# Attention block with Winograd-form projections on one core: when the small scale vectors are loaded, when the sums of staged tokens fall due, who scales B21 and B22, and the order of the products where output units change and end

## The chip, the cores and the metric

The kernel runs on 1 core of one Trainium2 chip, as one launch. The metric is the device time of a run in microseconds (us); less is better. The five engines are called by the names of the profile: PE (TensorE, matmuls), DVE (VectorE), ACT (ScalarE), POOL (GpSimd) and SP (SyncE, which issues most transfers).

## The reference, cut to what matters

One layer over x of 512 tokens by 2048 channels:

```
h    = rms_norm(x, norm_g)
proj = h @ w_in                     # 2048 x 8192: qa ka va ga | qb kb vb gb
ya   = stick_breaking_attention(qa, ka, va)          # 8 heads of 128, strictly causal
yb   = chunk_band_attention(qb, kb, vb, q_norm_g, k_norm_g, rel_bias)   # 8 heads, QK-norm
mixed = concat(ya * silu(ga), yb * silu(gb))
x    = x + mixed @ w_out            # 2048 x 2048
```

The channel gain norm_g is multiplied into x before the projection; the token's factor (1/rms) is multiplied in after it, as the row vector R.

## The kernel before

**Products.** All float32 values go to PE as two rounded parts, high and low, and each product is three matmuls (`three`, L463 to L465: high by high, then the two mixed ones). The projection is cut into 32 units of 256 columns; a unit walks the 2048 channels in 4 steps (`steps_`; a step has two channel tiles of 128, so tokens j = 2r and 2r+1). The output stage is 4 more units (NU to NU+3) of 8 steps, each with two token halves a = 0 and 1. Units 0 and 1, and unit NU, are PLAIN: 8 products of a 2x2 block scheme for each step. All others take 7 products in Winograd's form (`WINOGRAD`), which need sums of weights (`sums`, L331 to L335) and sums of tokens (T1 to T4, L428 to L433). The first eight steps are unit 0 and 1 in turn: steps 0, 1 read tokens j = 0, 1; steps 2, 3 read j = 2, 3; steps 4, 5 read j = 4, 5; steps 6, 7 read j = 6, 7. Unit 2 begins with step 8, and it is the first to read T1 to T4.

**Staging of tokens.** `activations(j)` loads tokens j into one of four stage tiles (`STAGE[j % 4]`, named cq, ck, cv, cg; j + 4 waits until the four sums of j have been read out of it), as two transfers: B11 with B12, and B21 with B22. `raw` scales each piece by the channel gain `ng_t` (ACT, L446), `raw_split` makes the high part (ACT, L457) and the low part (DVE, L458). Then the sums are made in one tile `xt` (L428, L430, L431) and split (L432, L433).

**Weights.** `step_weights(n)` loads the two 256 KB halves of step n (L292) into one of three buffers; `split` makes the high part on ACT (L351, `wh`) and the low part on DVE (L355, `wl`), in two buffers each: the high part of step n waits until PE has passed step n - 2. Part 0 has 1024 columns, part 1 (the sums) 768.

**Statistics and head scales.** `x_stats` loads x again in 16 tiles of 256 KB (L727) and squares them on ACT (L732); R follows from it. `constants` loads the head gains qg_t and kg_t (L1067, L1068) and scales qg_t on DVE (L1071).

**Order.** Every engine's order is written out at build time: an event loop (`schedule`) holds a clock and a cost for each operation, and each engine that is free takes the ready operation with the earliest due time. `need(k, d)` is due d us before PE would reach product k. On the chip each engine runs its list in order, so one instruction that waits holds all behind it.

**Ends of units.** `combine` puts a unit's seven sums together: copy of halves 0 and 1 to U (ACT, L606), then on DVE L613, L615, L617 (512 wide), L618, L617, L618; in the last unit (NU+3) also the residual x from `xres` (four operations of 256 between). Each of these frees a PSUM half-bank, and PE's next unit waits for those that it writes. In the output stage the two halves use fixed banks, so unit u + 1 writes where unit u has just been summed. The last two steps of NU+3 run, for each a, first 7 products of step 6, then 7 of step 7 (order `LAST`).

Of the kernel before, what the change touches and what calls it, by code (L numbers as in the profile page):

```python
# [8 lines left out]
F32 = mybir.dt.float32  # L9
# [6 lines left out]
P = 128  # L16
# [40 lines left out]
def trunk_kernel(ctx: ExitStack, tc: tile.TileContext, xT, xn, wi, wqk, wo, ng, qg, kg, rel, out):  # L57
# [189 lines left out]
    for n, (u, r) in enumerate(steps_):  # L247
        names = PLAIN if plain(u, r) else LAST if r == (NR if u < NU else NJ) - 1 else WINOGRAD
        if n == 0:

            for kk in range(2):
                put(n, 0, [x + ((kk,),) for x in names])
        elif u < NU:
            put(n, 0, names)
        elif u == NU + 3 and r > NJ - 3:

            if r == NJ - 1:
                for a in range(2):
                    for n_ in (n - 1, n):
                        put(n_, a, names if n_ == n else WINOGRAD)  # L260
        elif r in (0, NJ - 1):

            for a in range(2):
                put(n, a, names)
        else:
            for x in names:
                for a in range(2):
                    put(n, a, (x,))
# [118 lines left out]
    def activations(j, mixed):  # L387

        if mixed:
            g = j // 2 * 2  # L390
            yield lambda: (("store", g, j % 2) in done and ("store", g + 1, j % 2) in done
                           and position[0] > at_step[step_of[NU - 1, j // 2]] + 6)
            yield lambda: all(emptied(t_, NG - 1) for t_ in STAGE[:2]) if j % 2 == 0 else ("scores", 2 * NG - 1) in done
            k = at_step[step_of[NU, j]]
            kt = at_step[step_of[NU + plain(NU, j), j]]
        else:
            k = at_step[step_of[0, j // 2]] + (len(PLAIN) if j == 1 else 0)
            kt = at_step[step_of[2, j // 2]]
        lot = ("stage", j % 2 if mixed else j % 4)
# [23 lines left out]
        if not mixed:  # L423
# [4 lines left out]
        yield DV(512, lambda: dve.tensor_tensor(out=two(t[:, :2 * H]), in0=r[:, None, 3 * H:].to_broadcast([P, 2, H]),  # L428
                                               in1=two(r)[:, 0:3:2, :], op=ALU.subtract), need(kt, 4))
        yield DV(256, lambda: dve.tensor_tensor(out=t[:, 2 * H:3 * H], in0=t[:, :H], in1=r[:, 2 * H:3 * H], op=ALU.subtract), need(kt, 4))  # L430
        yield DV(256, lambda: dve.tensor_tensor(out=t[:, 3 * H:], in0=t[:, 2 * H:3 * H], in1=r[:, H:2 * H], op=ALU.add), need(kt, 4))  # L431
        yield AC(1024, lambda: act.copy(f(h[:, 3:]), t), need(kt, 2.6))  # L432
        yield DV(1024, lambda: dve.tensor_tensor(out=f(l[:, 3:]), in0=t, in1=f(h[:, 3:]).bitcast(F32), op=ALU.subtract), need(kt, 0.5))  # L433
        done.update(("x", j, x, mixed) for x in ("T1", "T2", "T3", "T4"))
# [6 lines left out]
    def raw(j, mixed, load_, r, k, parts, channels, scaled):  # L441
        yield load_
        if scaled:
            for x in parts:
                s_ = r[:, x[0] * H:x[1] * H]
                yield AC((x[1] - x[0]) * H, lambda: act.activation(s_, s_, AF.Copy, scale=ng_t[:, channels:channels + 1]), need(k, 3.5))  # L446
        done.add(("scaled", j, channels, mixed))
        for x in parts:
            spawn(raw_split(j, mixed, r, k, *x), (0, 0, j))
# [136 lines left out]
    def combine(u, a):  # L586
# [27 lines left out]
        free(4)  # L614
        yield DV(256, lambda: dve.tensor_tensor(out=c[0][:, 0], in0=w[0], in1=w[1], op=ALU.add), soon(1))  # L615
        yield there(2, 3)
# [6 lines left out]
        if u == NU and PLAIN_STEPS:  # L623
            yield there(5)
            yield DV(256, lambda: add_(c[1][:, 1], c[1][:, 1], v(one(5))), soon(1))
            free(5)
        final = u == NU + 3
        if final:

            yield lambda: ("xres", a) in done  # L630
            xf = [xres[a].rearrange("p h (b f c) -> p h b f c", f=2, c=P)[:, :, :, f, :] for f in range(2)]
            where = lambda h: out[(2 * h + a) * P:(2 * h + a + 1) * P, (u - NU) * S:(u - NU + 1) * S]
            def both_x():
                sub_(w[1], w[1], xf[0][:, 1])
                add_(w[0], w[0], xf[1][:, 0])

            def add_x():
                add_(c[0][:, 0], c[0][:, 0], xf[0][:, 0])
                add_(c[1][:, 1], c[1][:, 1], xf[1][:, 1])

            yield DV(256, both_x, soon(0.5), n=2)
            yield DV(256, add_x, soon(0.8), n=2)
        yield there(6)
# [70 lines left out]
    def x_stats():  # L714
        yield lambda: position[0] > 12
        for t in range(NT):
# [340 lines left out]
    def constants():  # L1057
# [76 lines left out]
```

## Time and profile before

| what | value |
|---|---|
| time, median of 3 runs | 960.51 us (960.45 to 961.32) |
| profiled execution: its own time | 961.33 us |
| profiled execution: span from first to last instruction | 959.5 us |
| PE busy | 934.9 us, 97% |
| DVE busy | 825.2 us, 86% |
| ACT busy | 583.0 us, 61% |
| POOL busy | 19.0 us, 2% |

The profile is of one execution; times in it count from its first instruction. A matmul of 256 columns shows as 0.28 us, but the next starts 0.12 us after it, since they are pipelined: the pitch, from start to start, is what counts. In step 0 the pitch is 0.21 us.

### The profile page before, as it was taken

The page shows a single profiled execution, that of the slowest core. Times are in us where ns is not written, and L with a number is a line of the kernel's source. Part 1 is how long each engine was busy: PE and PEld are TensorE (multiplying, and loading weights), DVE is VectorE, ACT ScalarE, POOL GpSimd, SP SyncE. Part 2 cuts the span into 40 slices and gives each one's busy share as a digit, 9 for nine tenths or more (in the row PEclk, how much of TensorE's full clock was granted, in tenths as well). Part 3 has the DMA queues.
Part 4 walks back from the last instruction along what each step waited for, and adds up shares of the span by engine and source line. Part 5 has one row for each costly group of instructions (what it writes and reads, how often), then busy time and mean ns, then how long its engine had stood idle before and what let it go on. Part 6 is the DMA issues. An engine that isn't in the chain of part 4 may idle for free.

```text
span 959.5 us, 19478 instructions
## 1 busy us (share of the span) xinstructions
PE 934.9 (97%) x7592; PEld 923.2 (96%) x7592; DVE 825.2 (86%) x1519; ACT 583.0 (61%) x1104; POOL 19.0 (2%) x61
## 2 busy tenths in 40 slices
PE   5899999999999999999999999999999999999997
PEld 5899999999999999999999999999999999999997
DVE  4799998889999889889998898889989988777875
ACT  6876765865467658654776585547768666533332
POOL 0000000000000000000000000000000000101010
PEclk9999999999999999999999999999999999999998
DMA  6842233323322332133223332332322446656361
GB/s 230 261 136 78 88 110 121 100 67 111 110 90 88 116 106 88 68 132 98 89 79 122 110 100 66 120 101 88 100 88 89 144 132 202 151 195 178 110 178 45
DMA packets 63629, 112.43 MB, mean 117 GB/s; under 512 B 7216, under 2 KB 11312, under 8 KB 63536
## 3 DMA queue, kind: packets, MB, share of 16 engines
q1 hardware_dynamic: 61392, 107.51, 34.5%
q0 software_dynamic: 1728, 3.15, 2.0%
q8 instruction: 59, 0.97, 0.4%
q10 hardware_dynamic: 416, 0.52, 0.2%
q14 instruction: 34, 0.28, 0.1%
HBM read 102.77 MB, written 8.39 MB: 116 GB/s over the span
## 4 chain that ended last, share of the span: by engine, by line
PE 84%; DVE 9%; ACT 3%; DMA 2%; issue 1%; SPq 0%; DVEq 0%; ACTq 0%
PE banks L463 27%; PE banks L464 27%; PE banks L465 27%; DVE wl L355 3%; PE banks L952 2%; PE banks L880 1%; ACT wh L351 1%; DMA x<-mixd 1%; DMA wt<-in_wi 1%; PE banks L988 1%; DMA qg_t<-in_qg 1%; DVE wt L331 0%; DVE c L976 0%; DVE U L617 0%; DVE wtl L961 0%
## 5 line engine op out<-in xcount | busy, mean ns | idle before, releaser
L463 PE MATMUL banks<-xh,wh 128*128 128x256 f32 x1776 | 512.2, 288 | 9.1 <-ACT xh L457 8.3
L464 PE MATMUL banks<-xl,wh 128*128 128x256 f32 x1776 | 504.0, 284 | 5.1 <-DVE xl L458 5.0
L465 PE MATMUL banks<-xh,wl 128*128 128x256 f32 x1776 | 503.8, 284 | 0.0
L351 ACT CAST wh<-wt 128x1024 fp32r<-128x1024 f32 (+2 forms) x306 | 285.7, 943 | 255.1 <-PE banks L464 146.6
L355 DVE TENSOR_TENSOR wl<-wt,wh 128x1024 fp32r<-128x1024 f32 (+2 forms) x306 | 331.5, 1087 | 72.5 <-ACT wh L351 68.6
L463 PEld LDWEIGHTS banks<-xh,wh 128*128 128x128 f32 x1776 | 341.4, 192 | 10.3 <-ACT xh L457 8.5
L464 PEld LDWEIGHTS banks<-xl,wh 128*128 128x128 f32 x1776 | 341.6, 192 | 6.4 <-DVE xl L458 5.9
L465 PEld LDWEIGHTS banks<-xh,wl 128*128 128x128 f32 x1776 | 341.4, 192 | 0.3 <-DVE wl L355 0.3
L463 PE MATMUL banks<-wh,xh 128*128 128x256 f32 x432 | 122.7, 284 | 1.7 <-DVE co L618 1.7
L464 PE MATMUL banks<-wl,xh 128*128 128x256 f32 x432 | 122.3, 283 | 0.1
L465 PE MATMUL banks<-wh,xl 128*128 128x256 f32 x432 | 122.2, 283 | 0.0
L331 DVE TENSOR_TENSOR wt<-wt 128x512 f32<-128x512 f32 x144 | 98.1, 682 | 13.8 <-DMA wt<-in_wo 13.8
L463 PEld LDWEIGHTS banks<-wh,xh 128*128 128x128 f32 x432 | 82.9, 192 | 2.5 <-DVE co L618 2.5
L464 PEld LDWEIGHTS banks<-wl,xh 128*128 128x128 f32 x432 | 82.9, 192 | 0.3 <-DVE wl L355 0.3
L465 PEld LDWEIGHTS banks<-wh,xl 128*128 128x128 f32 x432 | 82.9, 192 | 0.0
L334 DVE TENSOR_TENSOR wt<-wt 128x256 f32<-128x256 f32 x144 | 60.3, 420 | 2.0
L335 DVE TENSOR_TENSOR wt<-wt 128x256 f32<-128x256 f32 x144 | 60.4, 419 | 2.0
L606 ACT COPY U<-banks 128x512 f32<-128x512 f32 x36 | 21.1, 585 | 25.4 <-PE banks L465 25.0
L961 DVE TENSOR_TENSOR wtl<-banks,wth 128x128 fp32r<-128x128 f32 (+1 forms) x64 | 30.8, 482 | 1.4 <-ACT wth L960 1.0
L952 PE MATMUL banks<-ident,W 128*128 128x128 f32 x160 | 28.6, 276 | 1.4 <-DVE wtl L961 0.9
L960 ACT CAST wth<-banks 128x128 fp32r<-128x128 f32 (+1 forms) x64 | 26.9, 422 | 3.2 <-PE banks L952 3.1
L617 DVE TENSOR_TENSOR U<-banks,c 128x512 f32<-128x512 f32 x30 | 20.7, 688 | 7.8 <-PE banks L465 6.1
(179 smaller groups left out, 1019.2 us busy)
## 6 DMA issues: line engine op xcount, KB each, us to landing
wt<-in_wi SPq DMA_DIRECT2D x256, 256.0 KB, 2.9
wt<-in_wo SPq DMA_DIRECT2D x64, 256.0 KB, 3.4
xs<-in_xn SPq DMA_DIRECT2D x16, 256.0 KB, 4.3
mixd<-c SPq DMA_DIRECT2D x16, 256.0 KB, 2.1
out<-co SPq DMA_DIRECT2D x16, 256.0 KB, 4.6
x<-in_xT SPq DMA_DIRECT2D x14, 256.0 KB, 5.4
co<-in_xn POOLq DMA_DIRECT2D x12, 256.0 KB, 7.2
bias<-in_rel SPq DMA_DIRECT2D x8, 256.0 KB, 3.6
```

Of the source, the lines that this page charges most:

```text
L331: yield DV(512, lambda: dve.tensor_tensor(out=some(t, 8, -7, 2), in0=some(t, 5, -5, 2), in1=some(t, 1, 0, 2), op=ALU.add), need(k0, 4))
L334: yield DV(256, lambda: dve.tensor_tensor(out=some(t, 9, 2), in0=some(t, 8, 2), in1=some(t, 0, 2), op=ALU.add), need(k1, 4))
L335: yield DV(256, lambda: dve.tensor_tensor(out=some(t, 12, 1), in0=some(t, 9, 2), in1=some(t, 4, 2), op=ALU.add), need(k1, 3.5))
L351: act.copy(whl[n, part][0][:, c], t)
L355: yield DV(c.stop - c.start, lambda: dve.tensor_tensor(out=l[:, c], in0=t, in1=h[:, c].bitcast(F32), op=ALU.subtract), need(k, 0.5))
L463: pe.matmul(o, lh, rh, start=start, stop=False, **kw)
L464: pe.matmul(o, lh, rl, start=False, stop=False, **kw)
L465: pe.matmul(o, ll, rh, start=False, stop=stop, **kw)
L606: act.copy(x[0], pair(u, a, 0, 1))
L952: pe.transpose(t[:, j * P:(j + 1) * P], src[:, j * P:(j + 1) * P], ident)
L960: yield AC(w, lambda: act.copy(th[:, blocks, :], tv))
L961: yield DV(w, lambda: dve.tensor_tensor(out=tl[:, blocks, :], in0=tv, in1=th[:, blocks, :].bitcast(F32), op=ALU.subtract))
```

## The change

Six edits:

1. `x_stats` may start when PE has passed 36 products, not 12; `constants` loads the head gains when PE has passed 40, not at once.
2. The sums of tokens j < 4 are due 8 us before the step of unit 0 that needs the stage tile again (step 4 or 6), not before unit 2.
3. B21 and B22 of tokens j = 2 to 7 in the projection are scaled by DVE (`tensor_scalar`, 512 wide), not by ACT: six instructions.
4. The first step of units NU+1 to NU+3 runs in the order `FIRST`: of each seven products those to halves 0, 1, 4, 2, 3, 7, 6, where it was 0, 1, 2, 7, 3, 6, 4.
5. The last two steps of NU+3 take turns product by product, both in the order `LAST`, for a = 0 and then a = 1.
6. At the end of NU+3, for a = 1, the sum of L615 and the residual of that quarter go to POOL (`apart`). The wait for `xres` in the builder is gone.

```
+FIRST = tuple(WINOGRAD[i] for i in (0, 1, 6, 2, 4, 3, 5))
-        names = PLAIN if plain(u, r) else LAST if r == (NR if u < NU else NJ) - 1 else WINOGRAD
+        names = PLAIN if plain(u, r) else LAST if r == (NR if u < NU else NJ) - 1 else FIRST if u > NU and r == 0 else WINOGRAD
...
                 for a in range(2):
-                    for n_ in (n - 1, n):
-                        put(n_, a, names if n_ == n else WINOGRAD)
+                    for x in LAST:
+                        for n_ in (n - 1, n):
+                            put(n_, a, (x,))
...
-            kt = at_step[step_of[2, j // 2]]
+            kt, dt = (at_step[step_of[0, j // 2 + 2]], 8) if j < 4 else (at_step[step_of[2, j // 2]], 0)
...
+                if x[2] == ("B21", "B22") and j > 1:
+                    yield DV((x[1] - x[0]) * H, lambda: dve.tensor_scalar(out=s_, in0=s_, scalar1=g_, scalar2=None, op0=ALU.mult), need(k, 3.5))
+                else:
+                    yield AC((x[1] - x[0]) * H, lambda: act.activation(s_, s_, AF.Copy, scale=g_), need(k, 3.5))
...
+        if final and a:
+            spawn(apart(c, w, xf), (0, 0))
+        else:
+            yield DV(256, lambda: dve.tensor_tensor(out=c[0][:, 0], in0=w[0], in1=w[1], op=ALU.add), soon(1))
...
             def add_x():
-                add_(c[0][:, 0], c[0][:, 0], xf[0][:, 0])
+                if not a:
+                    add_(c[0][:, 0], c[0][:, 0], xf[0][:, 0])
                 add_(c[1][:, 1], c[1][:, 1], xf[1][:, 1])
...
+    def apart(c, w, xf):
+        yield G(0.75, lambda: pool.tensor_tensor(out=c[0][:, 0], in0=w[0], in1=w[1], op=ALU.add), clock[0])
+        done.add("c11")
+        yield G(0.75, lambda: pool.tensor_tensor(out=c[0][:, 0], in0=c[0][:, 0], in1=xf[0][:, 0], op=ALU.add), clock[0])
+        done.add("c11 x")
...
-        yield lambda: position[0] > 12
+        yield lambda: position[0] > 36
...
+        yield lambda: position[0] > 40
         def gains():
```

In the sums' five operations every `need(kt, d)` became `need(kt, dt + d)`. The line numbers of the changed kernel are larger: L458 became L466, L355 became L358, L428 to L431 became L432 to L435, L615 became L629, L617 became L631, L618 became L632, L1071 became L1095.

**Where instructions moved.** DVE in step 0, before. The tile x_111 is the stage tile of tokens 0, xt_161 their sums, wl_0 the low part of step 0's weights:

```order
L428 TENSOR_TENSOR xt_161<-x_111 128x512
L1071 TENSOR_SCALAR qgs<-qg_t 128x1
L458 TENSOR_TENSOR xl_113<-x_111,xh_112 128x512
L355 TENSOR_TENSOR wl_0_143<-wt_124,wh_0_142 128x512
L430 TENSOR_TENSOR xt_161<-xt_161,x_111 128x256
L458 TENSOR_TENSOR xl_116<-x_114,xh_115 128x256
```

The scale of qg_t is second of the six. DVE in step 0 of the change:

```order
L432 TENSOR_TENSOR xt_159<-x_111 128x512
L466 TENSOR_TENSOR xl_113<-x_111,xh_112 128x512
L358 TENSOR_TENSOR wl_0_143<-wt_124,wh_0_142 128x512
L434 TENSOR_TENSOR xt_159<-xt_159,x_111 128x256
L466 TENSOR_TENSOR xl_116<-x_114,xh_115 128x256
L466 TENSOR_TENSOR xbqk_145<-x_114,xbqk_145 128x256
```

The scale of qg_t, which stood ahead of the low parts of B21 and B22 (xl_113) and of the second half of step 0's weights, has gone from here.

It stands now behind the low part of step 5's weights. DVE of the change there (xt_438 are the sums of tokens 3, xt_520 those of tokens 4, x_439 is the stage tile of tokens 6):

```order
L358 TENSOR_TENSOR wl_5_472<-wt_314,wh_5_471 128x1024
L1095 TENSOR_SCALAR qgs<-qg_t 128x1
L437 TENSOR_TENSOR xl_122<-xt_438,xh_121 128x1024
L432 TENSOR_TENSOR xt_520<-x_293 128x512
L452 TENSOR_SCALAR x_439<-x_439,ng_t 128x512
L466 TENSOR_TENSOR xl_441<-x_439,xh_440 128x256
L466 TENSOR_TENSOR xbwth_351<-x_439,xbwth_351 128x256
L434 TENSOR_TENSOR xt_520<-xt_520,x_293 128x256
```

Behind it stand the pieces of tokens 6 and 7, which step 6 reads: from the scale of qg_t to the low part of B11 of tokens 7 (exclusive) there are three instructions of 1024 columns, five of 512 and four of 256.

SP before, from step 2's weights (wt_146) on; xs is a tile of the statistics:

```order
L292 DMA wt_146<-in_wi 128x512 x2
L1067 DMA qg_t<-in_qg 128x1
L1068 DMA kg_t<-in_kg 128x1
L292 DMA wt_184<-in_wi 128x512 x2
L727 DMA xs<-in_xn 128x512
L292 DMA wt_234<-in_wi 128x512 x2
L727 DMA xs<-in_xn 128x512 x2
```

The loads of the head gains stand right behind the weights of step 2. SP of the change, from the second load of tokens 5 (x_362) to the weights of step 8 (wt_501):

```order
L420 DMA x_362<-in_xT 128x512
L295 DMA wt_417<-in_wi 128x512 x2
L749 DMA xs<-in_xn 128x512
L419 DMA x_439<-in_xT 128x2x256
L420 DMA x_439<-in_xT 128x512
L749 DMA xs<-in_xn 128x512 x2
L1091 DMA qg_t<-in_qg 128x1
L1092 DMA kg_t<-in_kg 128x1
L295 DMA wt_501<-in_wi 128x512 x2
```

The loads of the weights of steps 3 to 7 and of tokens 4 to 6 (x_293, x_362, x_439) now stand ahead of that of qg_t, and three tiles of the statistics too.

DVE at the end of NU+3, for a = 1, before:

```order
L613 TENSOR_TENSOR co_1_11764<-banks,U 128x2x128
L615 TENSOR_TENSOR co_1_11764<-U 128x2x128
L617 TENSOR_TENSOR U<-banks,co_1_11764 128x512
L618 TENSOR_TENSOR co_1_11764<-banks,U 128x2x128
L617 TENSOR_TENSOR U<-U,xres_10452 128x256
L618 TENSOR_TENSOR U<-U,xres_10452 128x256
L618 TENSOR_TENSOR co_1_11764<-co_1_11764,xres_10452 128x2x128 x2
L617 TENSOR_TENSOR co_1_11764<-banks,U 128x2x128
L618 TENSOR_TENSOR co_1_11764<-banks,U 128x2x128
```

For each a there are ten operations on DVE. In the change, the same place:

```order
L621 TENSOR_TENSOR co_1_11754<-banks,U 128x2x128
L631 TENSOR_TENSOR U<-banks,co_1_11754 128x512
L632 TENSOR_TENSOR co_1_11754<-banks,U 128x2x128
L631 TENSOR_TENSOR U<-U,xres_10451 128x256
L632 TENSOR_TENSOR U<-U,xres_10451 128x256
L632 TENSOR_TENSOR co_1_11754<-co_1_11754,xres_10451 128x2x128
L631 TENSOR_TENSOR co_1_11754<-banks,U 128x2x128
L632 TENSOR_TENSOR co_1_11754<-banks,U 128x2x128
```

Two of the ten are gone from here, L615 and one of the two that add xres to co. POOL of the change, from its last transfers on:

```order
L683 DMA co_1_10835<-in_xn 128x512 x2
L683 DMA co_0_11276<-in_xn 128x512 x2
L683 DMA co_1_11309<-in_xn 128x512 x2
L674 TENSOR_TENSOR co_1_11754<-U 128x2x128
L676 TENSOR_TENSOR co_1_11754<-co_1_11754,xres_10451 128x2x128
```

The two stand there as L674 and L676, alone behind the transfers of NU+1 and NU+2.

## Rows read from the trace of the kernel before

**Rows 1.** The page, part 1: busy us of each engine, its share of the span, and its instructions.

```profile
PE 934.9 (97%) x7592; PEld 923.2 (96%) x7592; DVE 825.2 (86%) x1519; ACT 583.0 (61%) x1104; POOL 19.0 (2%) x61
```

**Rows 2.** Who waited for whom, for PE over the whole span: total us, times, longest.

```profile
PE banks L463 <- ACT xh L457: 8.3, 2, 5.8
PE banks L464 <- DVE xl L458: 5.0, 2, 4.8
PE banks L463 <- DVE co L618: 1.7, 4, 0.6
PE banks L463 <- DVE c L617: 0.8, 1, 0.8
```

**Rows 3.** The timeline of 0 to 22 us, lines of PE, ACT, DVE and SP's queue (SPq): start, duration, engine, line, operation, and in brackets the idle time ahead of it and who ended it.

```profile
5.84 0.58 PE L463 MATMUL banks<-xh,wh 128*128 128x256 f32 x1 [5.84 <-ACT xh L457]
...
6.98 0.41 PE L465 MATMUL banks<-xh,wl 128*128 128x256 f32 x1
...
7.02 0.60 ACT L457 CAST xh<-x 128x512 fp32r<-128x512 f32 x1
...
8.52 0.33 SPq L1067 DMA_DIRECT2D qg_t<-in_qg  x1
...
9.11 0.41 PE L463 MATMUL banks<-xh,wh 128*128 128x256 f32 x1
...
13.56 0.15 DVE L1071 TENSOR_SCALAR qgs<-qg_t 128x1 f32<-128x1 f32 x1 [6.08 <-DMA qg_t<-in_qg]
13.63 0.68 DVE L458 TENSOR_TENSOR xl<-x,xh 128x512 fp32r<-128x512 f32 x1
...
14.37 0.58 PE L464 MATMUL banks<-xl,wh 128*128 128x256 f32 x1 [4.84 <-DVE xl L458]
...
19.40 0.28 PE L464 MATMUL banks<-xbqk,wh 128*128 128x256 f32 x1
...
21.07 0.28 PE L463 MATMUL banks<-xh,wh 128*128 128x256 f32 x1
```

**Rows 4.** The timeline of PE over step 4, whose first matmul is at 38.35 and which ends where step 5 begins at 48.70; and one line of the table by stretches (length, busy us of PE, PEld, DVE, ACT, POOL, then PE's granted clock, DMA share, GB/s).

```profile
38.35 0.28 PE L463 MATMUL banks<-xh,wh 128*128 128x256 f32 x1
...
41.37 0.38 PE L463 MATMUL banks<-xh,wh 128*128 128x256 f32 x1 [2.50 <-ACT xh L457]
...
48.70 0.28 PE L463 MATMUL banks<-xh,wh 128*128 128x256 f32 x1
...
43.30:46.70 3.40, 3.40 (x18) 3.40 (x18) 1.66 (x3) 3.38 (x8) 0.00 (x0) 0.50 0.95 293
```

**Rows 5.** The same table for 58 to 115 us and 140 to 200 us (same columns), and from the timeline DVE's copy that makes R.

```profile
58.00:115.00 57.00, 56.55 (x461) 55.66 (x460) 56.83 (x106) 37.74 (x71) 0.77 (x4) 1.00 0.30 93
...
140.00:200.00 60.00, 59.69 (x492) 58.99 (x491) 52.92 (x118) 38.99 (x100) 0.96 (x6) 1.00 0.32 102
...
67.70 0.68 DVE L764 COPY R<-banks 128x512 f32<-128x512 f32 x1
```

**Rows 6.** Transfers issued in 0 to 60 us: line, count, KB of each, median us from issue to landing.

```profile
x<-in_xT SPq DMA_DIRECT2D x14, 256.0 KB, 5.4
...
ng_t<-in_ng SPq DMA_DIRECT2D x1, 8.0 KB, 2.2
qg_t<-in_qg SPq DMA_DIRECT2D x1, 0.5 KB, 5.0
```

**Rows 7.** Groups of instructions with shapes kept apart: busy us, mean ns of one, idle ahead.

```profile
L458 DVE TENSOR_TENSOR xl<-x,xh 128x512 fp32r<-128x512 f32 x12 | 8.2, 685 | 0.1
...
L856 DVE TENSOR_TENSOR W<-banks,W 128x128 f32<-128x128 f32 x8 | 2.3, 286 | 0.1
...
L752 DVE TENSOR_SCALAR diag<-ident,rstd 128x128 f32<-128x128 f32 x4 | 1.2, 302 | 0.0
```

**Rows 8.** The timeline where unit NU+2 follows NU+1 (its first product is at 869.09), lines of PE and DVE; and the table by stretches for the first step and the next of NU+2, and for the first step of NU+3 (columns as in rows 4).

```profile
869.09 0.28 PE L463 MATMUL banks<-wh,xh 128*128 128x256 f32 x1
...
870.97 0.38 PE L463 MATMUL banks<-wh,xh 128*128 128x256 f32 x1 [0.64 <-DVE co L618]
...
873.96 0.39 PE L463 MATMUL banks<-wh,xh 128*128 128x256 f32 x1 [0.23 <-DVE co L618]
...
870.50 0.74 DVE L618 TENSOR_TENSOR co<-banks,U 128x256 f32<-128x256 f32 x2
...
873.50 0.41 DVE L618 TENSOR_TENSOR co<-banks,U 128x256 f32<-128x256 f32 x1
...
869.10:875.50 6.40, 5.53 (x44) 5.13 (x43) 6.26 (x13) 2.49 (x3) 2.62 (x3) 1.00 0.32 53
...
910.80:917.20 6.40, 5.54 (x45) 5.13 (x44) 6.25 (x13) 2.48 (x3) 2.63 (x3) 1.00 0.40 77
```

**Rows 9.** The timeline of the end of the run, lines of ACT, DVE and PE, and POOL's one elementwise instruction of 128 columns at the start.

```profile
950.87 0.59 ACT L606 COPY U<-banks 128x512 f32<-128x512 f32 x1 [4.45 <-PE banks L465]
...
952.35 0.28 PE L465 MATMUL banks<-wh,xl 128*128 128x256 f32 x1
...
952.51 0.69 DVE L617 TENSOR_TENSOR U<-banks,co 128x512 f32<-128x512 f32 x1
...
955.25 0.41 DVE L618 TENSOR_TENSOR co<-banks,U 128x256 f32<-128x256 f32 x1
...
1.02 0.29 POOL L1049 TENSOR_SCALAR_AFFINE_SELECT ident<-ident 128x128 f32<-128x128 f32 x1
```

More of the change, by code (lines that the diff above doesn't have):

```diff
@@ L394, in activations @@
             k = at_step[step_of[NU, j]]
-            kt = at_step[step_of[NU + plain(NU, j), j]]
+            kt, dt = at_step[step_of[NU + plain(NU, j), j]], 0
         else:
             k = at_step[step_of[0, j // 2]] + (len(PLAIN) if j == 1 else 0)
-            kt = at_step[step_of[2, j // 2]]
+            kt, dt = (at_step[step_of[0, j // 2 + 2]], 8) if j < 4 else (at_step[step_of[2, j // 2]], 0)
         lot = ("stage", j % 2 if mixed else j % 4)
@@ L428, in activations @@
         yield DV(512, lambda: dve.tensor_tensor(out=two(t[:, :2 * H]), in0=r[:, None, 3 * H:].to_broadcast([P, 2, H]),
[L429 to L433, printed above, removed]
+                                               in1=two(r)[:, 0:3:2, :], op=ALU.subtract), need(kt, dt + 4))
+        yield DV(256, lambda: dve.tensor_tensor(out=t[:, 2 * H:3 * H], in0=t[:, :H], in1=r[:, 2 * H:3 * H], op=ALU.subtract), need(kt, dt + 4))
+        yield DV(256, lambda: dve.tensor_tensor(out=t[:, 3 * H:], in0=t[:, 2 * H:3 * H], in1=r[:, H:2 * H], op=ALU.add), need(kt, dt + 4))
+        yield AC(1024, lambda: act.copy(f(h[:, 3:]), t), need(kt, dt + 2.6))
+        yield DV(1024, lambda: dve.tensor_tensor(out=f(l[:, 3:]), in0=t, in1=f(h[:, 3:]).bitcast(F32), op=ALU.subtract), need(kt, dt + 0.5))
         done.update(("x", j, x, mixed) for x in ("T1", "T2", "T3", "T4"))
@@ L445, in raw @@
                 s_ = r[:, x[0] * H:x[1] * H]
-                yield AC((x[1] - x[0]) * H, lambda: act.activation(s_, s_, AF.Copy, scale=ng_t[:, channels:channels + 1]), need(k, 3.5))
+                g_ = ng_t[:, channels:channels + 1]
+                if x[2] == ("B21", "B22") and j > 1:
+                    yield DV((x[1] - x[0]) * H, lambda: dve.tensor_scalar(out=s_, in0=s_, scalar1=g_, scalar2=None, op0=ALU.mult), need(k, 3.5))
+                else:
+                    yield AC((x[1] - x[0]) * H, lambda: act.activation(s_, s_, AF.Copy, scale=g_), need(k, 3.5))
         done.add(("scaled", j, channels, mixed))
@@ L614, in combine @@
         free(4)
-        yield DV(256, lambda: dve.tensor_tensor(out=c[0][:, 0], in0=w[0], in1=w[1], op=ALU.add), soon(1))
+        final = u == NU + 3
+        xf = [xres[a].rearrange("p h (b f c) -> p h b f c", f=2, c=P)[:, :, :, f, :] for f in range(2)] if final else None
+        if final and a:
+            spawn(apart(c, w, xf), (0, 0))
+        else:
+            yield DV(256, lambda: dve.tensor_tensor(out=c[0][:, 0], in0=w[0], in1=w[1], op=ALU.add), soon(1))
         yield there(2, 3)
@@ L626, in combine @@
             free(5)
-        final = u == NU + 3
         if final:
-            yield lambda: ("xres", a) in done
-            xf = [xres[a].rearrange("p h (b f c) -> p h b f c", f=2, c=P)[:, :, :, f, :] for f in range(2)]
             where = lambda h: out[(2 * h + a) * P:(2 * h + a + 1) * P, (u - NU) * S:(u - NU + 1) * S]
+            yield lambda: not a or "c11" in done
             def both_x():
@@ L637, in add_x @@
             def add_x():
-                add_(c[0][:, 0], c[0][:, 0], xf[0][:, 0])
+                if not a:
+                    add_(c[0][:, 0], c[0][:, 0], xf[0][:, 0])
                 add_(c[1][:, 1], c[1][:, 1], xf[1][:, 1])
             yield DV(256, both_x, soon(0.5), n=2)
-            yield DV(256, add_x, soon(0.8), n=2)
+            yield DV(256, add_x, soon(0.8), n=2 - a)
         yield there(6)
@@ L652, in combine @@
         if final:
+            yield lambda: not a or "c11 x" in done
             yield from stored(lambda: sp.dma_start(where(0), t[:, 0, :]))
```

## The prediction

> **What bounds the kernel now.** I read the page's busy times first. PE is busy 97% of the span, DVE 86%, POOL hardly [rows 1]; a change that leaves PE's products alone, as this one does, can only win PE's idle time, its time at half clock, and what lies before its first and behind its last matmul. The span is 959.5 us, the profiled execution 961.33, its median fellow 960.51; sums below are made on the span, and I carry them to the median as they stand.
>
> Then the view of who PE waited for [rows 2]. The longest, 5.8, is the first; 4.8 of the 5.0 at DVE's L458, and 2.5 (8.3 less 5.8), are two more long ones; four of 1.7 in all are for DVE at L618, and one of 0.8 for L617.
>
> *Step 0* [rows 3]. DVE sits idle 6.08 us for the 0.5 KB of qg_t, issued at 8.52, while the high part of B21 is there at 7.62. PE's last matmul ahead of the stop starts at 9.11 and takes 0.41, so it runs out at 9.5; it resumes at 14.37. Its pitch is 0.21 us until 19.40, then 0.12: the lower and the upper of the two clock levels, 1.2 and 2.4 GHz. The rise comes 5.0 us after PE resumed. Step 1 begins at 21.07, 15.23 us after the first matmul, where 48 matmuls at 0.12 are 5.76.
>
> *Step 4* [rows 4]. 38.35 to 48.70 is 10.35 us, so 4.59 are lost: 2.50 waiting for tokens 5, and then 3.4 us in which the granted clock is 0.50, about 1.7 lost; the rest is restart.
>
> *58 to 115 us* [rows 5]. DVE is busy 56.83 of 57 us there, and PE 56.55: a second engine without slack. This decides whether time won earlier can be kept.
>
> *Output stage* [rows 8]. The first step of NU+2 takes from 869.09 to 875.50, 6.41 us where 42 matmuls are 5.04, and so does that of NU+3: 1.37 lost in each. *End* [rows 9]: the last matmul starts at 952.35, DVE's last operation at 955.25, the span ends at 959.5.
>
> **Step 0: the wait removed.** qg_t's scale leaves this place, so the low part of B21 follows L428 as soon as its high part is there, at about 7.7, and the low part of the second half of the weights right behind it. PE needs the first at 9.5. So PE runs on from 5.84 at 0.21 until the clock rises. When is an estimate: 5.0 us after a resumption in step 0, 5.3 in step 4 (41.37 to 46.7) [rows 3, 4], which counted from 5.84 to 6.98 gives 10.8 to 12.3; I take 11.6. By then PE has done 2 + (11.6 - 6.98)/0.21, about 24 matmuls, and step 1 begins at 11.6 + 24 x 0.12 = 14.5 instead of 21.07: **6.5 us** (5.9 to 6.9). ACT's and DVE's lists for tokens 0 and 1 are otherwise unchanged.
>
> **Step 4.** With 14.5 for step 1, steps 2 to 6 are due at 20.3, 26.0, 31.8, 37.5, 43.3. Tokens 5 now load behind the weights of step 6 and not behind tiles of the statistics. Those weights need the buffer of step 3, whose low part waits for PE to pass step 1: two casts of 1024 columns, at most 2.4 us by twice the 512-wide ones [rows 3, 7], so 22.7; the tokens are issued at 23.7 to 24.6 and land 5.4 later by the median [rows 6], 29.1 to 30.0. Two short ACT operations and one of DVE make 31. PE asks at 32.1. The loss goes: **4.6 us**; if they land 2.5 us later it is 3, or less if the clock falls too.
>
> **The new place of qg_t.** The load stands behind the weights of step 7, which need step 4's buffer (PE past step 2 at 26.0, plus 2.4: 28.4), and six more issues of about 0.5: issued near 31.9. It lands 2.2 to 5.0 later, as ng_t and qg_t did [rows 6]: 34.1 to 36.9. DVE reaches it behind step 5's low part, 31.8 + 2.4 = 34.2. So DVE waits 0 to 2.7 us with the pieces of tokens 6 and 7 behind it. The twelve operations between cost 8 to 9 us (0.69 at 512 columns and 0.29 at 128 [rows 7], linear between and beyond, less the overlap); with no wait the low part of tokens 7 starts near 42.7, and step 6 asks for it at 43.7. A wait of 1.8, the middle, costs PE **0.8 us**; the ends are 0, and 1.8 with 1.7 of half clock as in step 4, 3.5.
>
> **Scaling by DVE, sums due earlier.** Six operations of 512 columns go to DVE. At 128 columns a tensor_scalar shows 302 ns and a two-tensor operation 286 [rows 7], so I price them like the latter, 6 x 0.69 = 4.1 us at most. They fill idle time: the wait of 6.08 is gone, and the sums of tokens 0 to 3 move into the first 40 us, which PE's slow start left idle on DVE. At nothing on the path; if that cover failed, 4.1.
>
> **Can PE stay ahead?** In 58 to 115 DVE is full [rows 5], but by what it has put off, not by what the stretch itself asks. With the 6.1 idle us at qg_t gone and R, with the first heads' work, moved behind step 12, I count DVE ahead of its weights through step 24. The 0.8 wait at L617 in that stretch [rows 2] should mostly go: **0.6** (0 to 0.8). The heads of group 0 then fall where DVE is busy 52.9 of 60 us and ACT 39.0 [rows 5]; I take **-0.3** for new short waits (0 to -2).
>
> **First steps of NU+2 and NU+3.** PE's fourth product (half 7) waits until 870.97 for the last operation of a = 0 (two L618 from 870.50), and that of a = 1 until 873.96 for the L618 at 873.50 [rows 8]. In FIRST half 7 comes sixth, two products of 0.36 later, and half 4 third, whose bank L613 freed long before. DVE's list there is the same, so its ends stay: after 873.96 two products are left, not four, and the step ends 0.72 to 0.82 earlier. Two steps: **1.6 us** (0.9 to 1.7, if DVE's ends move). NU+1 follows a unit without a combination and has no such loss.
>
> **End.** Now step 6 and 7 finish a half together every 0.72 us, counted back from PE's end E: halves 0, 1 at E - 3.6, half 4 at E - 2.16, half 3 at E - 1.44. The 512-wide L617 can start near E - 1.4, where it starts at 952.51 = E - 0.1 now, and two operations of the ten on DVE are gone, one of them behind it (0.33). That is **1.6 us** at most, and I take **1.5**. It holds if POOL is in time: L617 overwrites U, so it waits for POOL's sum, which can start at E - 2.9 when U is copied. It has 1.5 us. POOL's 128-column operation takes 0.29 [rows 9]; 256 columns with a second input lie between 0.4 and 1.2, I take 0.7, and the second sum has two more us. If it took 2.5, 1.0 would be lost.
>
> The Trainium skill speaks against this part: "GPSIMD Engine Reference", "3.1 Elementwise — side-by-side cycle accounting", has a two-input fp32 addition at about twice VectorE's time (4497 ns for 2048 columns). No run here shows a two-input operation on POOL; by that figure 256 columns are an estimated 0.6 to 0.9 us, L617 would not be delayed, and the sum stays.
>
> **Sum.** 6.5 + 4.6 - 0.8 + 0.6 - 0.3 + 1.6 + 1.5 = 13.7 us, so 945.8 of span and 946.8 at the median.
>
> **Rivals.**
>
> *A. The wait moves with the load.* qg_t lands at 37 or later, DVE stands for 3 us, PE waits 2 us or more in step 6 and the clock falls as it did in step 4. For it: the load is issued behind eight transfers of 256 KB, and landed 5.0 us late in such a crowd. Against: PE's demand there is a step later. It costs 4 more: 951. Chance 0.18.
>
> *B. DVE gives nothing back.* The full stretch [rows 5] holds PE to a lead of about 4 us, and only step 4's loss or step 0's is kept. Gain 4 + 1.6 + 1.5, less 0.5: 954. For: 56.83 of 57 busy, and 4.1 us of work added. Against: the put-off sums are done by then. Chance 0.10.
>
> *C. Slower: the heads of group 0 come too late.* R is made at 67.70 now [rows 5]; its tiles load behind step 7's, so it comes some 17 us later, near step 13. The four tiles of group 0 must be read before unit 4, 16 steps in, can be summed, or PE stands with full banks. The chain of two heads has about 15 us to spare at step 20; it decides from 15 + 13.7, that is if the chain came 29 us late. At 35 the time is 967. Chance 0.03.
>
> *D. The edits do less than they say:* the clock in step 0 rises no earlier, since the start is not dense enough, and PE runs at 0.21 through step 0 and 1 (+4 us): 951. Against: PE worked from 5.84 to 9.5 without a stop of more than a matmul's length. Chance 0.07.
>
> **How the numbers follow.** The forecast has 0.62: 946.8, its own range 943.5 (all upper ends) to 949.5. A and D at 951 add 0.25, B at 954 is left at the edge. The range **943.5 to 953** leaves out B, C and little more. About 0.2%, 1.9 us, is what a measurement of this kernel tells from no change: faster 0.94, within 0.03, slower 0.03.
>
> **What would show it.** Right: no idle time of DVE ahead of the scale of qg_t in step 0; step 1 near 14.5, step 5 near 37.5; one step of 5.5 to 5.7 us at the start of NU+2 and NU+3; from the last matmul's start to the span's end 5.6 us, now 7.2. Wrong: DVE idle over 3 us near 34 and PE with it (A); PE short of weights between steps 8 and 16 (B); waits of PE near step 20 (C); a pitch of 0.21 beyond 13 us (D); L617 waiting for POOL.

## Result, and the profile after

The changed kernel takes 948.85 us (median of 4 runs, 948.39 to 951.60) where the kernel before takes 960.62 (4 runs, 960.45 to 961.32): a ratio of 0.988, 95% interval 0.9868 to 0.9893, so 11.8 us less. The forecast was 946.8, with a range of 943.5 to 953. The profiled execution took 948.75 us, with a span of 947.0 where it was 959.5; the profiled execution before, with 961.33, was the slowest of its four, so spans differ by 0.8 us more than the medians.

The page's busy times, to hold against [rows 1]: PE's are 3.8 us less, and fewer matmuls run at the longer pitch; the other 8.7 of the span's 12.5 us were idle time of PE.

```profile
PE 931.1 (98%) x7592; PEld 920.3 (97%) x7592; DVE 827.0 (87%) x1523; ACT 579.6 (61%) x1097; POOL 20.4 (2%) x63
```

Who PE waited for, over the whole span (total us, times, longest), to hold against [rows 2]:

```profile
PE banks L471 <- ACT xh L465: 7.2, 2, 5.8
PE banks L974 <- DVE wtl L983: 0.9, 3, 0.3
PE banks L473 <- DVE wl L358: 0.8, 1, 0.8
PE banks L472 <- DVE xl L466: 0.5, 2, 0.3
PE banks L471 <- DVE co L632: 0.4, 2, 0.2
```

The waits of 4.8 for DVE's low part and of 0.8 for L617 are gone; those for L618 (now L632) shrank from 1.7 to 0.4. The ACT wait of 2.5 in step 4 is gone too; in its place stand one of 1.4 (7.2 less 5.8) and one of 0.8 for the low part of weights, and both are new and stand in step 6.

Step 0, from the timeline, PE and DVE (start, duration, engine, line, in brackets the idle time ahead and who ended it), to hold against [rows 3]:

```profile
5.83 0.58 PE L471 MATMUL banks<-xh,wh 128*128 128x256 f32 x1 [5.83 <-ACT xh L465]
...
7.65 0.69 DVE L466 TENSOR_TENSOR xl<-x,xh 128x512 fp32r<-128x512 f32 x1 [0.19 <-ACT xh L465]
...
9.52 0.41 PE L473 MATMUL banks<-xh,wl 128*128 128x256 f32 x1
...
10.80 0.29 PE L473 MATMUL banks<-xh,wl 128*128 128x256 f32 x1
...
14.16 0.28 PE L471 MATMUL banks<-xh,wh 128*128 128x256 f32 x1
```

The low part of B21 starts at 7.65, where it was 13.63. PE does not stop; its matmuls go from 0.41 to 0.28 us, and from a pitch of 0.21 to one of 0.12, at 10.8, where it was 19.4. Step 1 begins at 14.16, 6.91 earlier.

Step 5 begins at 37.20 (48.70 in [rows 4]), 11.50 earlier: step 4 loses nothing any more. Then step 6, which runs from 42.96; the lines of SP's queue, DVE and PE:

```profile
31.35 0.43 SPq L1091 DMA_DIRECT2D qg_t<-in_qg  x1
...
32.60 1.23 DVE L358 TENSOR_TENSOR wl<-wt,wh 128x1024 fp32r<-128x1024 f32 x1 [0.32 <-DMA xs<-in_xn]
...
38.65 0.15 DVE L1095 TENSOR_SCALAR qgs<-qg_t 128x1 f32<-128x1 f32 x1 [4.83 <-DMA qg_t<-in_qg]
...
44.19 0.38 PE L473 MATMUL banks<-xh,wl 128*128 128x256 f32 x1 [0.84 <-DVE wl L358]
...
45.99 0.38 PE L471 MATMUL banks<-xh,wh 128*128 128x256 f32 x1 [1.42 <-ACT xh L465]
...
46.66 0.39 PE L472 MATMUL banks<-xl,wh 128*128 128x256 f32 x1 [0.28 <-DVE xl L466]
...
52.04 0.28 PE L471 MATMUL banks<-xh,wh 128*128 128x256 f32 x1
```

The load of qg_t is issued at 31.35 and lands 7.3 us later; in that time the core's DMA engines are 0.95 busy. DVE, in order, stands 4.83 us in front of its 0.15 us of work, with the pieces of tokens 6 and 7 and the weights of step 6 behind it; PE stands three times, 2.54 us in all, and step 6 takes 9.08 us, 3.32 more than 48 matmuls at 0.12.

The stretch of 58 to 115 us, where DVE was busy 56.83 of 57 and PE 56.55 [rows 5] (columns as in rows 4):

```profile
58.00:115.00 57.00, 56.93 (x471) 56.38 (x470) 56.36 (x102) 40.24 (x68) 0.49 (x3) 1.00 0.39 122
```

DVE is still full there (56.36 us), and PE is busy all but 0.07 us: the full stretch does not hold PE back.

The first step of NU+2, which begins at 859.42, and the next, from PE's timeline (against [rows 8]), and the end, lines of POOL, DVE and PE (against [rows 9]):

```profile
859.42 0.28 PE L471 MATMUL banks<-wh,xh 128*128 128x256 f32 x1
...
864.30 0.39 PE L471 MATMUL banks<-wh,xh 128*128 128x256 f32 x1 [0.22 <-DVE co L632]
...
865.12 0.28 PE L471 MATMUL banks<-wh,xh 128*128 128x256 f32 x1
...
938.69 0.73 POOL L674 TENSOR_TENSOR co<-U 128x256 f32<-128x256 f32 x1 [30.13 <-ACT U L614]
...
939.50 0.74 POOL L676 TENSOR_TENSOR co<-co,xres 128x256 f32<-128x256 f32 x1
...
940.23 0.69 DVE L631 TENSOR_TENSOR U<-banks,co 128x512 f32<-128x512 f32 x1 [0.30 <-POOL co L676]
...
941.30 0.28 PE L473 MATMUL banks<-wh,xl 128*128 128x256 f32 x1
...
942.64 0.41 DVE L632 TENSOR_TENSOR co<-banks,U 128x256 f32<-128x256 f32 x1
```

That step takes 5.70 us, where it took 6.41. The 512-wide L617 (now L631) starts 1.07 us ahead of the last matmul, where it started 0.16 behind it; from the last matmul's start to the span's end it is 5.65 us, where it was 7.19.

### The profile page after: what moved, and what is told of

Read it like the earlier page. It is cut to its first block, busy times and chain, and to the rows that moved or that the text cites. A ratio compares the mean times of both kernels' runs of the same rounds, so it can differ in the third digit from the quotient of the medians.

```text
span 947.0 us, 19485 instructions
## 1 busy us (share of the span) xinstructions
PE 931.1 (98%) x7592; PEld 920.3 (97%) x7592; DVE 827.0 (87%) x1523; ACT 579.6 (61%) x1097; POOL 20.4 (2%) x63
## 4 chain that ended last, share of the span: by engine, by line
PE 91%; DVE 5%; DMA 1%; ACT 1%; issue 1%; SPq 0%; POOLq 0%; POOL 0%; DVEq 0%
PE banks L471 29%; PE banks L472 29%; PE banks L473 29%; DVE wl L358 2%; PE banks L974 2%; PE banks L902 1%; DMA qg_t<-in_qg 1%; DMA x<-in_xT 1%; PE banks L1010 1%; DVE c L998 0%; DVE co L632 0%; PE banks L847 0%; ACT wh L354 0%; DVE U L631 0%; DVE wtl L983 0%
## 5 line engine op out<-in xcount | busy, mean ns | idle before, releaser
L354 ACT CAST wh<-wt 128x768 fp32r<-128x768 f32 (+2 forms) x306 | 285.2, 942 | 241.9 <-PE banks L472 136.8
L358 DVE TENSOR_TENSOR wl<-wt,wh 128x768 fp32r<-128x768 f32 (+2 forms) x306 | 331.7, 1088 | 67.6 <-ACT wh L354 64.8
L334 DVE TENSOR_TENSOR wt<-wt 128x512 f32<-128x512 f32 x144 | 98.3, 683 | 11.3 <-DMA wt<-in_wo 10.8
L631 DVE TENSOR_TENSOR U<-banks,c 128x512 f32<-128x512 f32 x30 | 20.7, 688 | 8.0 <-PE banks L473 6.2
```

The source lines that it names most:

```text
L334: yield DV(512, lambda: dve.tensor_tensor(out=some(t, 8, -7, 2), in0=some(t, 5, -5, 2), in1=some(t, 1, 0, 2), op=ALU.add), need(k0, 4))
L354: act.copy(whl[n, part][0][:, c], t)
L358: yield DV(c.stop - c.start, lambda: dve.tensor_tensor(out=l[:, c], in0=t, in1=h[:, c].bitcast(F32), op=ALU.subtract), need(k, 0.5))
```

## The experiments

All are medians of 4 to 8 executions, and those of one kernel lie 0.6 to 2.6 us apart. In the twelve traces without the wait for qg_t in step 0 (all but those of the kernel before and ends_only), step 1 began between 13.6 and 15.4 us, as the pitch fell between 9.5 and 12.5. So a difference between medians of under some 1.5 us is read only where the traces show the step that it comes from. The theory going in: the forecast's terms hold but for the wait at qg_t, which is worth 3.3. Its main rivals: DVE has no slack, so the time would be lost behind step 8 anyway; and the loss of step 4 ended for another reason than the later statistics.

**scale_apart: the load at its old place, the scale at its new one.** On the changed kernel:

```
-        yield lambda: position[0] > 40
-
         def gains():
...
         yield Op("SP", 0.94, gains, 25.0)
+        yield lambda: position[0] > 40
         yield DV(1, lambda: dve.tensor_scalar(out=qgs, ...
```

> The changed kernel with the head gains loaded at once, as in the kernel before (behind the weights of step 2), but scaled where the changed kernel scales them, when PE has passed 40 products. Theory (only DVE's place in its list matters; the two loads of 0.5 KB cost the queue 0.9 us and harm nobody): no wait in step 0 and none in step 6, about 945.5 to 946. Rival (the two loads delay the weights or tokens behind them): step 3 or 4 waits, 947 or more. Rival (the wait in step 6 is not for qg_t): 948.8.

Measured: 945.67 us, ratio 0.9845 (0.9831 to 0.9858), 3.2 under the change and the lowest median here (sa_nopool, below, has 945.79, which is not told apart from it). Steps 1 to 7 take 5.76 us each; of the waits of PE for ACT and DVE only these stand ahead of the heads' own:

```profile
PE banks L471 <- ACT xh L465: 5.8, 1, 5.8
...
PE banks L472 <- DVE xl L466: 0.2, 1, 0.2
```

So the wait at qg_t cost what the trace said (3.32 us in step 6), and time won ahead of step 8 is kept: rival B (DVE gives nothing back) is out.

**gains_80: load and scale later still.** On the changed kernel:

```
-        yield lambda: position[0] > 40
+        yield lambda: position[0] > 80
```

> The changed kernel with the head gains loaded when PE has passed 80 products, not 40. Theory (the 3.3 us that step 6 of the changed kernel loses are DVE's wait for qg_t and nothing else): no wait of PE between 40 and 50 us, step 7 begins at 48.7 and all later ones 3.3 us earlier; about 945.5 (945.0 to 946.2), and no execution 3 us longer than the others. Rival (DVE has no slack for it: PE is held by DVE's list in 58 to 115 us whatever comes before): gain under 1 us, 948 or more, with new waits of PE for DVE in steps 8 to 20. Rival (the wait moves along to where the load now stands): DVE idle for qg_t near step 10 or 11, 947 or more.

Measured: 948.20 us (0.9854 to 0.9884). Step 6 loses nothing (43.58 to 49.34, 5.76), but the load, issued at 60.80, again stands behind transfers of weights and statistics, takes 3.4 us, and DVE waits 1.42 us for it, now in a stretch where it has little to spare. Against scale_apart PE loses 0.66 us of that by step 12; the rest of the 2.5 us between the medians comes among the heads, which stand in another order, and has no cause shown. The third possibility was right in kind: a load and its use put off together take their wait along.

**g_only: the kernel before, with the head gains alone put off.**

```
+        yield lambda: position[0] > 40
+
         def gains():
```

> The kernel before with one edit: the head gains are loaded when PE has passed 40 products. Theory of the terms: step 0 gives its 6.9 us by this alone, so step 1 begins at 14.2; the statistics still load ahead of tokens 5, so step 4 still loses 4 to 5 us; and the load of qg_t stands behind the weights of step 8 with its scale behind step 5's low part, so DVE waits there 4 us or more and PE loses 2 to 4. About 957 (955 to 959). Rival (the loss of step 4 came from the late start and goes with it): step 5 begins near 37.5, about 952. Rival (the clock, not qg_t, holds step 0): step 1 begins at 18 or later, 960 or more.

Measured: 954.01 us, ratio 0.9931 (0.9918 to 0.9943), 6.7 less than before; expected were 955 to 959. Step 1 begins at 14.45: all of step 0's gain comes from this one line. Step 4 still loses:

```profile
34.75 0.58 PE L463 MATMUL banks<-xh,wh 128*128 128x256 f32 x1 [2.50 <-ACT xh L457]
...
39.98 0.15 DVE L1073 TENSOR_SCALAR qgs<-qg_t 128x1 f32<-128x1 f32 x1 [3.21 <-DMA qg_t<-in_qg]
```

The same 2.50 us as in [rows 4], and 4.29 lost in the step. DVE waits 3.21 us for qg_t here too, but PE loses nothing by it: held up in step 4, it begins step 6 at 47.55, 4.6 us later than in the change, while DVE is free again only 1.3 us later. That was the error in the expected number.

**sa_act: scale_apart, with ACT scaling all of B21 and B22** (edit 3 undone), and **sa_stats12: scale_apart with the statistics let in at 12 products** (the first half of edit 1 undone).

```
-                if x[2] == ("B21", "B22") and j > 1:
+                if x[2] == ("B21", "B22") and j > 99:
```

```
-        yield lambda: position[0] > 36
+        yield lambda: position[0] > 12
```

> The kernel of scale_apart with all B21 and B22 scaled by ACT again. Theory (these six operations lie in idle time on either engine): within 0.6 us of 945.7. Rival (ACT's list holds back tokens 5 or 7, as its two operations of about 0.5 us stand ahead of the casts): PE waits 0.5 to 2 us in step 4 or 6, 946.5 to 948. Rival (DVE's added 2.9 us cost later, where it is full): 944.5 or less.

> The kernel of scale_apart with the statistics let in again when PE has passed 12 products, not 36. Theory (the statistics' tiles ahead of tokens 5 made step 4's loss): PE waits 2 to 3 us in step 4 for tokens 5, the clock falls as it did before, 4 to 4.6 us are lost: about 950 (949 to 951). Rival (DVE's scaling of B21 and B22 ended that loss, the statistics don't matter): 945.7. Rival (earlier statistics bring R earlier and are worth something behind step 8): below 945.

Measured: sa_act 949.43 us (0.9865 to 0.9893), sa_stats12 947.07 (0.9837 to 0.9868). Both theories fell. Late statistics without DVE's scaling lose 1.1 us in step 4 and 3.6 in step 6; DVE's scaling with early statistics loses nothing in step 4 and 0.6 in step 6. With neither (g_only) step 4 loses 4.29 and step 6, which PE reaches late, nothing. So either edit takes most or all of step 4's loss away, but the late statistics without DVE's scaling lose 3.6 in step 6 instead. Lines of ACT, DVE, SP's queue and PE of sa_act, which lead to step 6:

```profile
34.86 0.63 ACT L754 ACTIVATE xs<-xs 128x512 f32<-128x512 f32 x1 [1.74 <-DMA xs<-in_xn]
...
36.18 1.03 ACT L436 CAST xh<-xt 128x1024 fp32r<-128x1024 f32 x1
...
37.24 1.23 DVE L437 TENSOR_TENSOR xl<-xt,xh 128x1024 fp32r<-128x1024 f32 x1 [2.41 <-ACT xh L436]
...
38.74 0.38 SPq L419 DMA_DIRECT2D x<-in_xT  x1
...
45.88 0.38 PE L471 MATMUL banks<-xh,wh 128*128 128x256 f32 x1 [1.54 <-ACT xh L465]
```

and the same places in scale_apart:

```profile
32.90 1.04 ACT L436 CAST xh<-xt 128x1024 fp32r<-128x1024 f32 x1
...
34.17 1.22 DVE L437 TENSOR_TENSOR xl<-xt,xh 128x1024 fp32r<-128x1024 f32 x1
...
35.60 0.43 SPq L419 DMA_DIRECT2D x<-in_xT  x1
```

In sa_act ACT stands 1.74 us in front of a square of the statistics whose tile has not landed; behind it in the list is the cast of the sums of tokens 3. The DVE operation that follows that cast, and then the load of tokens 7, come 3.1 us later. PE waits 1.54 us ahead of a matmul of step 6, and the granted clock is 0.51 from 47.6 to 51.1 us.

**sa_act_late: sa_act with edit 2 undone as well.**

```
-            kt, dt = (at_step[step_of[0, j // 2 + 2]], 8) if j < 4 else (at_step[step_of[2, j // 2]], 0)
+            kt, dt = (at_step[step_of[2, j // 2]], 0)
```

> The kernel of sa_act with the sums of tokens 0 to 3 due ahead of unit 2 again (edit 2 undone; beside DVE's scaling edit 2 moves no instruction at all, so it can only be told here). Theory (the due time is no term: DVE reaches the sums early in any case): as sa_act within 0.4 us. Rival (sums put off hold the stage tiles of tokens 4 and 5, so that these load late): PE waits 1 us or more in step 4, 947 or more.

Measured: 949.80 us (0.987 to 0.9898), not told apart from sa_act. Built from the changed kernel, the two due times give the very same program on every engine: in the change, edit 2 does nothing.

**sa_v23: scale_apart with DVE scaling tokens 2 and 3 alone.**

```
-                if x[2] == ("B21", "B22") and j > 1:
+                if x[2] == ("B21", "B22") and j in (2, 3):
```

> The kernel of scale_apart with DVE scaling B21 and B22 of tokens 2 and 3 alone, and ACT those of tokens 4 to 7. Theory (ACT's list is what is late): step 4 loses nothing, as ACT is free for the first sums; step 6 loses 2 to 3.5 us as in sa_act, 948 to 949. Rival (only the first two scalings matter, since they let tokens 4 load early and all that follows): 945.7. Rival (each of the three pairs gives a third): about 948 with part of the loss in step 4.

Measured: 947.23 us (0.984 to 0.9867), runs from 945.70 to 947.80. Steps 1 to 7 take 5.76 each, so the theory fell and its first rival holds there: for steps 4 to 7 the first two scalings matter alone. Tokens 4 are issued at 13.25, as in the change (13.69) and not as in sa_act (19.59). The trace is ahead of scale_apart's up to step 11 and falls back behind it, where the heads come in another order; the 1.5 us between the medians have no cause shown.

**sa_act_st128: sa_act with the statistics behind step 7**, and **sa_st128: the same on scale_apart.**

```
-        yield lambda: position[0] > 36
+        yield lambda: position[0] > 128
```

> The kernel of sa_act (all scaling on ACT) with the statistics let in when PE has passed 128 products, that is behind step 7. Theory (DVE's scaling is worth 3.8 us because ACT's list is in order and holds the squares of the statistics, which wait for their transfers, ahead of the cast of the sums that frees a stage tile): with no squares in the first eight steps, PE loses 0.5 us or less in steps 4 to 7 though ACT scales; if the later heads cost nothing, 945.5 to 946.5. Rival (the scaling on ACT itself is too long a chain for tokens 5 to 7): step 6 loses 3 us or more as in sa_act, 949. Rival C of the prediction (R some eight steps later, the heads of group 0 too late): no loss up to step 8, but PE stands near steps 24 to 32, 949 or more.

> The kernel of scale_apart with the statistics let in behind step 7 (128 products, where it is 36): what a later R costs by itself. Theory (the heads of group 0 have time): 945.7, within 0.6. Rival C of the prediction (too late): PE stands near steps 24 to 32, 947 or more. Rival (fewer transfers in the first steps help): below 945.

Measured: 980.92 us (ratio 1.0195 to 1.0223) and 979.34 (1.0178 to 1.0206): both slower than before. In sa_act_st128 step 4 still loses 1.04 us, but steps 5, 6 and 7 take 5.76: with no squares in ACT's list the 3.6 us of step 6 are gone, though ACT scales. That settles step 6; the 1.0 in step 4 remain with ACT's scaling alone. Then both pay for the late R. In sa_st128 (the wait of PE, DVE's copy, and the table by stretches, columns as in rows 4):

```profile
128.42 2.05 PE L781 MATMUL banks<-diag,ones 128*128 128x128 f32 x8 [11.52 <-DVE diag L774]
...
130.51 0.69 DVE L786 COPY R<-banks 128x512 f32<-128x512 f32 x1 [1.65 <-PE banks L781]
...
117.00:152.00 35.00, 10.88 (x34) 7.51 (x34) 19.07 (x40) 18.41 (x42) 0.64 (x4) 0.53 0.19 54
```

R comes at 130.51 where scale_apart has it at 77.31, and PE, which stands in step 20 from 116.9 on, works 10.88 of 35 us at a granted clock of 0.53. From R to PE's return at 152.3 it is 22 us; counted back from 116.9, R may come near 95 at the latest, an estimate, some 18 us later than it does.

**ends_only: the kernel before with edits 4, 5 and 6 alone**, their lines as in the diff of the change.

> The kernel before with edits 4, 5 and 6 alone (FIRST, the last two steps in turn, the sum and residual of a = 1 on POOL). Theory of the terms: the end of the run gives 1.5 us, the first steps of NU+2 and NU+3 0.7 each, 3.0 to 3.3 in all: 957.4 (957.1 to 957.8). Rival (these gains need the earlier start): under 1 us, 960. Rival (POOL costs time elsewhere): NU+1 or NU+2 slower.

Measured: 958.19 us, ratio 0.9973 (0.9963 to 0.9983): 2.5 less, where 957.1 to 957.8 were expected. In its trace the first steps of NU+2 and NU+3 give 0.72 each, and the end 1.55 (5.64 us are left from the last matmul's start), 3.0 in all, as the theory has it; its step 0 waited 5.51 us for qg_t and took 0.50 longer than in the profile before, which in the trace takes some of that back. The first step of NU+1 takes 5.04 us before and here: nothing was lost in it. A loss of 0.38 in the trace before that is not in this one stands in the third step of NU, where PE waits for the low part of weights:

```profile
792.95 1.23 DVE L355 TENSOR_TENSOR wl<-wt,wh 128x1024 fp32r<-128x1024 f32 x1 [0.53 <-ACT wh L351]
...
794.23 0.39 PE L464 MATMUL banks<-wl,xh 128*128 128x256 f32 x1
```

It is not in g_only's trace either, which has none of edits 4 to 6, so they are not shown to have ended it.

**sa_noturns: scale_apart with edit 5 undone**, and **sa_nopool: with edit 6 undone.** In sa_noturns POOL's sum is written out behind the operation that overwrites U, so one quarter of the last unit's second half is summed from other values; the operations are the same.

```
-                    for x in LAST:
-                        for n_ in (n - 1, n):
-                            put(n_, a, (x,))
+                    for n_ in (n - 1, n):
+                        put(n_, a, names if n_ == n else WINOGRAD)
```

```
-        if final and a:
+        if 0:
...
-                if not a:
+                if 1:
                     add_(c[0][:, 0], c[0][:, 0], xf[0][:, 0])
...
-            yield DV(256, add_x, soon(0.8), n=2 - a)
+            yield DV(256, add_x, soon(0.8), n=2)
...
```

> The kernel of scale_apart with the last two steps of NU+3 one after the other again for each a (edit 5 undone, edit 6 kept). Theory (the turns let DVE's 512-wide L617 start 1.2 us ahead of PE's end): from the last matmul's start to the span's end 6.6 to 7 us where it is 5.4, so 946.8 to 947.2. Rival (edit 6 made the end): within 0.3 of 945.7.

> The kernel of scale_apart with the sum and the residual of a = 1 back on DVE (edit 6 undone, the turns of edit 5 kept). Theory: two operations of about 0.35 us each come back to DVE's list behind PE's last products, so 0.3 to 0.7 us more: 946.2. Rival (the turns alone made the end, DVE would have waited for PE anyway): within 0.2 us of 945.7.

Measured: sa_noturns 947.96 us (0.985 to 0.9877), sa_nopool 945.79 (0.9832 to 0.986). From the last matmul's start to the span's end: 5.65 in scale_apart, 7.59 without the turns (6.6 to 7 were expected), 6.12 without POOL, and 7.19 in the kernel before, which has neither. So the turns alone give 1.07 of the 1.54 us; POOL's part is 0.47 by the traces and not visible in the medians. The 7.59 are no measure of the turns, since there POOL's sum stands at another place, and DVE waits for it and then runs beside POOL's second addition:

```profile
940.35 0.42 DVE L630 TENSOR_TENSOR U<-U,xres 128x256 f32<-128x256 f32 x1 [0.44 <-POOL co L673]
940.69 0.94 DVE L631 TENSOR_TENSOR U<-U,xres 128x256 f32<-128x256 f32 x1
```

## Where the prediction was right and where wrong, by its own steps

| term | forecast, us | traces, us | what the runs say |
|---|---|---|---|
| step 0 | 6.5 | 6.91 | right; g_only alone gives 6.62, and the twelve traces 5.7 to 7.5, by when the pitch fell |
| step 4 | 4.6 | 4.59 | size right, cause only in part |
| new place of qg_t | -0.8 | -3.32 | mis-sized; 3.2 between the medians of the change and scale_apart |
| step 7 to the start of NU | 0.6 - 0.3 | 1.11 | L617's wait of 0.8 is gone; no run says what gave the rest |
| third step of NU | none | 0.38 | PE's wait for weights is not in the trace; cause open |
| first steps | 1.6 | 1.43 | right, 0.71 and 0.72; NU+1 had none to lose, as forecast |
| end | 1.5 | 1.5 | right |
| sum | 13.7 | 12.6 | 11.8 between the medians |

The time lay in the range, but one term was mis-sized: the step that failed is the bound on the wait for qg_t. The forecast had the issue near 31.9 (it was 31.35) and DVE there at 34.2 (33.8), both close; it took 2.2 to 5.0 us for the transfer, the ends of [rows 6], and it took 7.3. That is rival A, with a wait of 4.83 us, at a price of 3.3; the clock did not fall in the trace, so it cost less than A's 951. The way from the wait to PE was right: with the forecast's 8.5 us of work behind the scale, DVE's start at 38.65 gives a loss of some 3.8 us (38.65 + 8.5 - 43.4, with PE asking 0.4 us after step 6 begins; an estimate), and 3.3 were lost. A slip stands beside it: 1.8 us is called the middle of 0 to 2.7, which is 1.35, and would have cost PE 0.35 by the same sum. The same 0.5 KB took 3.4 us in gains_80, 4.4 in g_only, 5.0 before and 7.3 here, and while it was under way the core's DMA engines were busy 0.78, 0.84, 0.85 and 0.95 of the time. One such row was no upper end for another place in the queue; what held this transfer among its neighbours of 256 KB, the rows do not show. By "SBUF — State Buffer", "The DMA setup-cost knee (why "@ 1 MiB" ≠ asymptote)" of the Trainium skill, a transfer pays about 2 us whatever its size; by that qg_t would have landed near 33.4 (an estimate), before DVE asked, and nothing would have been lost. The trace differs: 7.3 us.

The second failure cancelled out, and that was luck. "At nothing on the path" was wrong for edit 3, and the whole credit for step 4 went to edit 1. Edit 3 is worth 3.8 us with late statistics (949.43 to 945.67). Late statistics are worth 0.6 with DVE's scaling by the traces (step 6 of sa_stats12); the 1.4 between the medians (947.07 to 945.67) are within what the starts vary. The late statistics alone, to which the forecast gave the 4.6, leave 1.1 us in step 4 and bring up 3.6 in step 6; had edit 3 been worth nothing, as forecast, the change would have taken up to some 952.6 us (948.85 + 3.8, an estimate; the two losses of step 6 may overlap). What I missed is that the scalings on ACT stood not in its idle time, which its share of busy time (61%) suggests, but in an in-order list, ahead of the casts that free a stage tile, and with that the next load; the first two of the six matter for steps 4 to 7 (sa_v23). Where the work's place in a list feeds a loop of load, scale, sum and release, its duration is not its price.

Edit 2 was credited with filling idle time of DVE; in the change it moves nothing. Rivals B and D fell (scale_apart; step 1 at 14.16). Rival C did not come about, since R was 12 us later (79.85 against 67.70), not 17; but its mechanism is real, as sa_st128 shows: 33.7 us above scale_apart.

At the end, POOL's two additions took 0.73 and 0.74 where 0.7 was forecast. The forecast feared that L631 would wait for the first. The trace has DVE idle 0.30 us ahead of L631 and puts it down to the second, which ends at 940.24; but the last matmul of half 3, which L631 reads as well, ends at 940.14 (939.86 + 0.28), and in ends_only, sa_act and sa_v23 the same 0.29 us is put down to PE. So POOL cost L631 at most some 0.1 us.

## What to carry to other kernels

When a small load is put off to clear a place, put off its use as well, but not the load: issued early (scale_apart), its 5.0 us on the way passed with no wait of DVE or PE for it, while issued late its 3.4 to 7.3 us held DVE, which works in order, for 1.4 to 4.8 us. Before work on a half-idle engine is priced at nothing, follow what stands behind it in its list to the next buffer that comes free. And test a due time or a priority by the order it produces: a number in a planner that changes no instruction changes no time.

## What the runs showed of the hardware

When the clock rises after a start varies among kernels with nearly the same start: in the twelve traces in which PE begins at 5.8 to 7.0 us and runs on, the pitch went from 0.21 to 0.12 at 9.5 to 12.5 us. The rise is read from the pitch, as the table's clock column reads 1.00 from the span's start; 0.21 is also the pitch in sa_act where that column reads 0.51. Nor do waits of one total always cost the clock: step 6 of the change has 2.54 us of waits within 3.3 us and stays at full clock, step 6 of sa_act has one of 1.54 and falls to 0.51. One of the four executions of the change took 951.60 us at a mean granted clock of 0.995, the others 948.39 to 948.94 at 0.999 or 1.000; it has no trace, so whether the clock fell behind step 6 there is open.

In sa_noturns DVE's second addition of 256 columns from two SBUF tiles took 0.94 us where the one before it, begun at 940.35, took 0.42, while POOL's addition (940.39 to 941.35, 0.96 where the change has 0.74) ran beside it; beside DVE's L621, which reads one SBUF tile and PSUM, POOL took 0.74. "SBUF — State Buffer", "Who interferes with whom", of the Trainium skill has DVE with two SBUF inputs and GpSimd exclude each other at a shared port; these durations agree with it, as one case; no run was made to test it.
